# The attention's work list of a decoder trunk in segments: transposes, products with V and logits in twos, projection units behind them

## The chip, the cores and the metric

One core of a Trainium2 chip runs the whole trunk in one launch. The metric is the device time of one execution in microseconds (us). Of the kernel before there are three timed runs and one execution under the hardware profiler; the profile's times count from the start of its span.

## The reference

Two layers act on a residual stream `h` of 256 tokens by 1024 features in float32. Each layer is a half-step SwiGLU feed-forward, a token mixer and another half-step feed-forward, with RMS norms before and after each. Layer 0 mixes by a gated linear recurrence, layer 1 by an attention with forget gates, whose keys, values and gates come from the stream behind layer 0:

```python
def forgetting_attention(xq, w_q, w_o, k, v, c):
    q = (xq @ w_q).reshape(Bn, S, N_HEADS, HEAD_DIM).transpose(0, 2, 1, 3) * (HEAD_DIM ** -0.5)
    for blk in range(S // Q_BLOCK):
        ...
        logits = jnp.einsum('bhqd,bhkd->bhqk', q[:, :, q0:end], k[:, :, :end]).astype(jnp.float32)
        logits = logits + c[:, :, q0:end, None] - c[:, :, None, :end]
        ...
        p = jax.nn.softmax(logits, axis=-1).astype(v.dtype)
        outs.append(jnp.einsum('bhqk,bhkd->bhqd', p, v[:, :, :end]))
    ...
    return o @ w_o
```

There are 16 heads of 64, and two query blocks of 128 tokens: block 0 sees 128 keys, block 1 sees 256. Masking is causal. Every weight matrix is used once.

## The kernel before

The tokens stand in two tiles, 0 and 1, of 128 each. A float32 product is made of three products of rounded parts: each weight tile is split on its way in, its upper part by ScalarE (`whi`, line 173), the rest by VectorE (`wlo`, line 177), and TensorE then runs the three matmuls of lines 183 to 185 with 512 columns each. A weight tile of 128 by 1024 is an *item*: for each of the two token tiles it gives one *unit* of six such matmuls. SyncE issues the loads into five raw buffers; nine split tiles may exist at a time (`RAW`, `WB`). A helper, `prepare_next`, decides when an item's load and splits are written down, by estimated times and by how many items ahead they are.

TensorE's order is the order in which the program writes its instructions down (`manual_schedule` for that engine). The other engines' orders are chosen by the scheduler of the tile library, which takes instructions under `high_priority` first, unless one is held in program order.

In the attention of layer 1 this order is a list by hand, `ATT_ORDER` (line 1221), worked off at lines 1409 to 1415. An entry `0` or `1` is the next unit of that token tile: eight units a tile, in all, of the projection to Q (line 1209), with the four transposes that turn Q written two units later (`heads_T`, line 986), and then eight of the output projection (line 1211). An entry such as `l1` is the next step of the softmax of that token tile, made by `attention` (line 1129):

- `l`, `logits`: matmuls of K and Q on 64 rows (line 1151) into two banks, then on VectorE a reduction that adds the bias and finds the maximum (line 1160) and two small corrections (lines 1164, 1165), then on ScalarE the exponentials with their sums (line 1167). One call makes two groups; an odd call returns at once. A group is four heads of tile 0 or two heads of tile 1: 512 columns. I call the two groups of a call A and B.
- `n`, `norm`: on VectorE the reciprocal of the sums (line 1173) and the product with it (line 1174).
- `t`, `turn`: four transposes of a group on TensorE (line 1180) and a copy out of PSUM on ScalarE (line 1182).
- `v`, `values`: matmuls with V that fill 64 columns each (line 1194). With every eighth head the bank is read out by ScalarE (`oh`, line 1200) and VectorE (`ol`, line 1201); these feed the output projection.

Steps of the list are written down under `high_priority`. Logits use the two banks named `gt`, transposes the two named `tr`, V and the projections the four named `mm`. The last unit of a token tile's output projection is followed by `enter` (line 259): squares on ScalarE (line 205), the post-norm on VectorE (lines 272 and 285), both at high priority, and the next feed-forward's inputs by transposes of `h` (line 214).

## Time and profile before

| what | value |
|---|---|
| median of three runs | 985.26 us (984.47 to 985.72) |
| the profiled execution | 985.32 us, of which its span 983.6 us |
| TensorE matmuls | 975.0 us busy, 99% of the span |
| TensorE weight loads | 812.0 us, 83% |
| VectorE | 610.2 us, 62% |
| ScalarE | 528.1 us, 54% |
| GpSimd | 59.9 us, 6% |
| TensorE's granted clock over the span | 0.998 |

In the rows, PE is TensorE's matmuls, PEld its weight loads, DVE VectorE, ACT ScalarE, POOL GpSimd and SP SyncE. A timeline's row gives start, duration, engine, line, operation, output and inputs, shapes and count; matmuls overlap in the pipeline, so the distance of two starts tells more than a duration. A group's row gives after the bar the busy time in us, the mean of one in ns, and after the second bar the idle time of the engine just before these instructions. A float32 matmul on half of the array shows as two records.

### The profile page before, as it was taken

What the parts mean: (1) busy time and instruction counts of PE and PEld (TensorE: products, weight loads), DVE (VectorE), ACT (ScalarE), POOL (GpSimd) and SP (SyncE); (2) the same over time, 40 slices, a digit from 0 to 9 for tenths busy, and PEclk for the clock granted to TensorE, in tenths of its full rate; (3) what the DMA queues carried; (4) which work ended last, traced back from release to release, by engine and by line L of the source; (5) the groups of instructions that cost most, each with busy time, mean ns of one, the idle gap of its engine ahead of it and who ended that gap; (6) DMA issues with size and microseconds to landing.
All of it is one profiled execution on the core that took longest, in us unless ns stands there. A gap on an engine that the chain in (4) does not pass through costs nothing.

```text
span 983.6 us, 13267 instructions
## 1 busy us (share of the span) xinstructions
PE 975.0 (99%) x4863; PEld 812.0 (83%) x4863; DVE 610.2 (62%) x849; ACT 528.1 (54%) x749; POOL 59.9 (6%) x110
## 2 busy tenths in 40 slices
PE   9999999999999999999999999999999999999997
PEld 6888888898978888888899888888887788888886
DVE  6756554678997555554677455555487876555542
ACT  7545443568986544443555344444366855444431
POOL 2400000100002000000113000002020010000000
PEclk9999999999999999999999999999999999999999
DMA  8877665465346766665589767667772467666631
GB/s 290 276 256 245 226 212 192 151 201 162 113 129 201 237 212 209 219 206 189 131 178 307 238 211 214 213 216 237 220 252 85 131 204 235 214 212 214 208 114 43
DMA packets 102966, 196.84 MB, mean 200 GB/s; under 512 B 12974, under 2 KB 36886, under 8 KB 102774
## 3 DMA queue, kind: packets, MB, share of 16 engines
q1 hardware_dynamic: 100102, 188.95, 60.8%
q0 software_dynamic: 2192, 6.51, 2.3%
q8 instruction: 38, 0.62, 0.3%
q10 hardware_dynamic: 608, 0.53, 0.2%
q14 instruction: 26, 0.21, 0.1%
HBM read 182.32 MB, written 3.16 MB: 189 GB/s over the span
## 4 chain that ended last, share of the span: by engine, by line
PE 95%; DVE 2%; issue 2%; ACT 1%; DMA 0%; POOL 0%; POOLq 0%; ACTq 0%; DVEq 0%
PE mm L183 28%; PE mm L185 27%; PE mm L184 27%; PE mm L1023 2%; PE gt L761 2%; PE tr L525 1%; PE mm L1291 1%; PE mm L190 1%; PE mm L191 1%; PE mm L192 1%; DVE wlo L177 1%; PE gt L214 1%; ACT pe L1167 0%; DMA h<-in_x_dram 0%; PE mm L1194 0%
## 5 line engine op out<-in xcount | busy, mean ns | idle before, releaser
L177 DVE TENSOR_TENSOR wlo<-raw,whi 128x1024 fp32r<-128x1024 f32 (+5 forms) x329 | 395.8, 1208 | 265.6 <-ACT whi L173 263.5
L173 ACT ACTIVATE whi<-raw 128x1024 fp32r<-128x1024 f32 (+5 forms) x329 | 342.1, 1046 | 316.7 <-PE mm L185 245.7
L183 PE MATMUL mm<-whi,xhi 128*128 128x512 f32 (+1 forms) x768 | 301.1, 392 | 0.0
L185 PE MATMUL mm<-whi,xlo 128*128 128x512 f32 (+1 forms) x768 | 298.1, 388 | 0.3 <-DVE xlo L228 0.3
L184 PE MATMUL mm<-wlo,xhi 128*128 128x512 f32 (+1 forms) x768 | 298.0, 388 | 0.0
L185 PEld LDWEIGHTS mm<-whi,xlo 128*128 128x128 f32 x768 | 144.2, 188 | 30.7 <-DVE xlo L228 0.7
L183 PEld LDWEIGHTS mm<-whi,xhi 128*128 128x128 f32 x768 | 144.2, 188 | 30.1 <-issue 2.0
L184 PEld LDWEIGHTS mm<-wlo,xhi 128*128 128x128 f32 x768 | 144.3, 188 | 28.1 <-DVE wlo L177 0.3
L183 PE MATMUL mm<-whi,hhi 128*128 128x512 f32 x352 | 137.8, 392 | 0.0
L185 PE MATMUL mm<-whi,hlo 128*128 128x512 f32 x352 | 137.1, 389 | 0.0
L184 PE MATMUL mm<-wlo,hhi 128*128 128x512 f32 x352 | 137.0, 389 | 0.0
L185 PEld LDWEIGHTS mm<-whi,hlo 128*128 128x128 f32 x352 | 66.1, 188 | 13.7
L183 PEld LDWEIGHTS mm<-whi,hhi 128*128 128x128 f32 x352 | 66.1, 188 | 13.4
L184 PEld LDWEIGHTS mm<-wlo,hhi 128*128 128x128 f32 x352 | 66.1, 188 | 13.4
L510 DVE SCALAR_TENSOR_TENSOR prod<-mm,rstd,sil 128x512 f32<-128x512 f32 (+1 forms) x48 | 33.9, 706 | 39.4 <-PE mm L185 31.3
L498 ACT ACTIVATE sil<-mm,rstd 128x512 f32<-128x512 f32 (+1 forms) x48 | 31.2, 653 | 43.1 <-PE mm L185 34.8
L198 POOL TENSOR_SCALAR nv<-ss 128x1 f32<-128x1 f32 x22 | 9.7, 441 | 554.0 <-ACT junk L205 554.0
L529 ACT ACTIVATE hhi<-tr 128x512 fp32r<-128x512 f32 (+1 forms) x48 | 24.8, 558 | 13.2 <-PE tr L525 13.2
L205 ACT ACTIVATE junk<-mm 128x512 bf16<-128x512 f32 x24 | 14.3, 595 | 32.7 <-PE mm L185 32.7
L530 DVE TENSOR_TENSOR hlo<-tr,hhi 128x512 fp32r<-128x512 f32 (+1 forms) x48 | 29.2, 641 | 2.6 <-ACT hhi L529 2.6
L272 DVE TENSOR_TENSOR t<-mm,gb 128x512 f32<-128x512 f32 x24 | 16.2, 687 | 23.6 <-ACT junk L205 23.4
L190 PE MATMUL mm<-xhi,whi 128*126 128x256 f32 (+1 forms) x88 | 24.7, 281 | 0.0
(211 smaller groups left out, 918.6 us busy)
## 6 DMA issues: line engine op xcount, KB each, us to landing
raw<-in_ffn_w_down_dram SPq DMA_DIRECT2D x88, 512.0 KB
raw<-in_ffn_w_up_dram SPq DMA_DIRECT2D x80, 512.0 KB
raw<-in_ffn_w_gate_dram SPq DMA_DIRECT2D x78, 512.0 KB
prr<-prod SPq DMA_DIRECT2D x40, 256.0 KB
raw<-in_rg_w_in_dram SPq DMA_DIRECT2D x10, 504.0 KB
raw<-in_rg_w_out_dram SPq DMA_DIRECT2D x10, 504.0 KB
raw<-in_ffn_w_gate_dram SPq DMA_DIRECT2D x19, 256.0 KB
raw<-in_ffn_w_up_dram SPq DMA_DIRECT2D x16, 256.0 KB
```

What stands on the lines that cost most here:

```text
L173: up = nc.scalar.activation(hi[:parts, c:c + m], rawv[:, c:c + m], AF.Copy)
L177: nc.vector.tensor_tensor(lo[:parts, c:c + m], rawv[:, c:c + m], hi[:parts, c:c + m].bitcast(F32), ALU.subtract)
L183: nc.tensor.matmul(ps, xh, wh, start=first, stop=False)
L184: nc.tensor.matmul(ps, xh, wl, start=False, stop=False)
L185: nc.tensor.matmul(ps, xl, wh, start=False, stop=last)
L190: nc.tensor.matmul(ps, wh, xh, start=first, stop=False)
L498: nc.scalar.activation(s[:, :nn], ps, AF.Silu, scale=rs[t][:, 0:1])
L510: nc.vector.scalar_tensor_tensor(pr[:, :nn], ps, rs[t][:, 0:1], s, ALU.mult, ALU.mult)
L529: nc.scalar.activation(hv, tp[:, :nn], AF.Copy)
L530: nc.vector.tensor_tensor(lv, tp[:, :nn], hv.bitcast(F32), ALU.subtract)
L761: nc.tensor.matmul(ps[j][:w, g * S:(g + 1) * S], wv[rows, o:o + w], xc[rows, k, :], start=start, stop=stop, skip_group_check=True)
L1023: nc.tensor.matmul(ps[:, j * S:(j + 1) * S], w, x, start=k == 0 and j == 0 and i == 0, stop=k == 7 and i == 2, skip_group_check=True)
```

## The change

Only the list is another; the entries are as many of each kind as before.

```diff
-    ATT_ORDER = ("0 0 0 0 0 0 0 l0 0 1 n0 l0 1 1 t0 n0 1 l0 v0 1 t0 n0 l0 1 v0 n0 1 t0 l1 1 v0 t0 n1 l1 0 v0 "
-                 "n1 l1 t1 0 n1 l1 t1 0 n1 l1 v1 v1 t1 0 n1 l1 t1 0 n1 l1 v1 v1 t1 0 n1 l1 t1 0 n1 v1 v1 0 t1 1 "
-                 "t1 v1 1 v1 1 1 1 1 1 1")
+    ATT_ORDER = ("0 0 0 0 0 0 0 l0 l0 0 1 1 n0 1 n0 1 t0 t0 l0 l0 1 1 n0 1 n0 1 t0 t0 v0 v0 l1 l1 0 n1 0 n1 "
+                 "t1 t1 v0 v0 l1 l1 0 n1 0 n1 t1 t1 v1 v1 l1 l1 0 n1 0 n1 t1 t1 v1 v1 l1 l1 0 n1 0 n1 "
+                 "t1 t1 v1 v1 1 1 v1 v1 1 1 1 1 1 1")
```

A segment of the new list is: two transposes, two steps with V, two entries of logits, then projection units with the two norms among them. In the middle of the list a step with V belongs to groups that were transposed one segment earlier.

## The prediction

> **What bounds the kernel now.** I read the page first, then the groups of the attention's stretch, then the stretches by engine, then the timelines of TensorE, VectorE and ScalarE side by side. The page says what the end hangs on:

> ```profile
> span 983.6 us, 13267 instructions
> ...
> PE 95%; DVE 2%; issue 2%; ACT 1%; DMA 0%; POOL 0%; POOLq 0%; ACTq 0%; DVEq 0%
> ```

> The chain that ended last is TensorE for 95% of the span. The groups of lines between 724 and 792 us, where the attention's list is worked off, show whether the steps that the change moves ever hold TensorE up (last column: idle time just before them):

> ```profile
> L1180 PE MATMUL tr<-ident,pe 128*128 128x128 f32 x48 | 7.4, 277 | 0.0
> L1194 PE MATMUL mm<-pT,v 128*64 128x128 f32 x96 | 7.3, 283 | 0.0
> L1151 PE MATMUL gt<-kT,qT 64*128 64x256 f32 x32 | 4.5, 402 | 0.0
> ```

> They never do: the 48 transposes, the products with V and the logits waited 0.0 us in total. The other engines are not idle there, though. In the ten microseconds from 765 the columns are length, then busy time of TensorE, its weight loads, VectorE, ScalarE and GpSimd:

> ```profile
> 765.00:775.00 10.00, 10.00 (x79) 7.89 (x76) 10.00 (x31) 8.54 (x18) 0.00 (x0) 1.00 0.60 192
> ```

> VectorE is busy for all ten, ScalarE for 8.54, and yet TensorE does not stop. So this stage is bound by TensorE's own instruction stream, and the softmax on the two other engines is hidden behind it because the list leaves it time. There are two ways for a new order to move the time: TensorE's stream itself gets shorter, or the cover of the softmax is lost.

> **Part 1: what TensorE's stream gains.** The order list decides TensorE's order alone, and the counts stay as they are. I take the price of a change between full-array work and work on half the array (logits: 64 rows, V: 64 columns) from a V step that stands alone, and of transposes from a lone one:

> ```profile
> 775.14 0.40 PE L185 MATMUL mm<-whi,ol 128*128 128x512 f32 x1
> 775.47 1.20 PE L1194 MATMUL mm<-pT,v 128*64 128x128 f32 x16
> 776.60 0.50 PE L183 MATMUL mm<-whi,oh 128*128 128x512 f32 x1
> 776.93 0.40 PE L184 MATMUL mm<-wlo,oh 128*128 128x512 f32 x1
> ...
> 777.86 0.39 PE L185 MATMUL mm<-whi,ol 128*128 128x512 f32 x1
> 778.09 0.60 PE L1180 MATMUL tr<-ident,pe 128*128 128x128 f32 x4
> 778.45 0.48 PE L183 MATMUL mm<-whi,oh 128*128 128x512 f32 x1
> 778.76 0.39 PE L184 MATMUL mm<-wlo,oh 128*128 128x512 f32 x1
> ```

> From 777.86 to 778.76 are two projection products (0.227 each, the pitch of 777.86 to 778.09) and four transposes: 0.90 - 0.454 = 0.446, or 0.11 a transpose. Transposes mixed in among products cost nothing beyond themselves. From 775.14 to 776.93 are two products and eight matmuls with V (sixteen records): 1.79 - 0.454 = 1.336; at 0.109 each the eight take 0.87, so a stretch of half-array work pays about 0.46 for going in and out. The 0.33 from 776.60 to 776.93, 0.10 more than a product's pitch, is part of it. TensorE's order before has eleven such stretches, after it eight, with four seams between V and logits inside them both times. Three fewer at 0.4 to 0.46: **-1.3 us**. Grouping the transposes in twos gains nothing. The two `l` entries that now stand together are one step as before, since the odd one returns at once.

> [...]

> **Part 2: what the softmax loses.** With two groups A and B of a logits step, the list of before puts the transposes of A behind the next logits step, those of B another unit later. One step of token tile 1, in the three engines:

> ```profile
> 752.59 1.14 PE L1151 MATMUL gt<-kT,qT 64*128 64x256 f32 x8
> 753.65 0.50 PE L183 MATMUL mm<-whi,xhi 128*128 128x512 f32 x1
> ...
> 759.46 0.66 PE L1180 MATMUL tr<-ident,pe 128*128 128x128 f32 x4
> ...
> 761.77 0.60 PE L1180 MATMUL tr<-ident,pe 128*128 128x128 f32 x4
> ```
> ```profile
> 753.06 0.69 DVE L1174 TENSOR_TENSOR pe<-pe,sm 128x512 f32<-128x512 f32 x1
> 753.75 0.43 DVE L1160 CUSTOM_DVE_ANT_0 pe<-gt,bias 128x256 f32<-128x256 f32 x1
> ...
> 756.91 0.69 DVE L1174 TENSOR_TENSOR pe<-pe,sm 128x512 f32<-128x512 f32 x1
> 758.17 0.17 DVE L1173 RECIPROCAL sm<-sm 128x2 f32<-128x2 f32 x1 [0.57 <-ACT pe L1167]
> 758.37 0.69 DVE L1174 TENSOR_TENSOR pe<-pe,sm 128x512 f32<-128x512 f32 x1
> ```
> ```profile
> 756.58 0.58 ACT L1182 ACTIVATE pT<-tr 128x512 f32<-128x512 f32 x1
> 757.06 0.50 ACT L1167 ACTIVATE pe<-pe,mx 128x256 f32<-128x256 f32 x1
> ```

> The logits start at 752.59 and end at 753.73; VectorE's first reduction starts at 753.75, 1.16 after the logits began. A is ready at 756.91 + 0.69 = 757.60, 3.85 after that first reduction, so 5.01 after the logits began. Its transposes came at 759.46: 1.86 to spare. B is ready at 758.37 + 0.69 = 759.06, its transposes came at 761.77: 2.71 to spare. That slack is the cover.

> In the new list every step of tile 1 reads: two transposes, two V, logits, then `0 n1 0 n1`, then the transposes of these same logits. Between logits and transposes stand two units of six products. TensorE reaches them 1.06 (752.59 to 753.65) + 0.33 + 11 x 0.227 = **3.89** after the logits began, against 5.01. The built order confirms that VectorE still does reductions A, B, A, B and ScalarE exponentials A, A, B, B, but now without the copy of a transposed tile (756.58 to 757.06, 0.48) between A and B, so B is ready 759.06 - 757.60 - 0.48 = 0.98 after A. By segment:

> - A segment with nothing in the way (the third of tile 1): A waits 5.01 - 3.89 = 1.12. Then come 0.45 of transposes; B waits 0.98 - 0.45 - 0.10 = 0.43. I add 0.1 for each wait, for the pipeline that has to fill again (nearest row: the 0.10 behind the V step above; bounds 0 and 0.3). Sum **1.8**.
> - The second segment: a V step that completes four heads' pairs stands right before the logits, and its evacuation stands ahead of the reductions in VectorE's order. In before it took this:

> ```profile
> 758.51 0.60 ACT L1200 ACTIVATE oh<-mm 128x512 fp32r<-128x512 f32 x1 [0.37 <-PE mm L1194]
> ```
> ```profile
> 759.14 0.69 DVE L1201 TENSOR_TENSOR ol<-mm,oh 128x512 fp32r<-128x512 f32 x1
> 759.75 0.41 DVE L1160 CUSTOM_DVE_ANT_0 pe<-gt,bias 128x256 f32<-128x256 f32 x1
> ```

>   From 758.51 to 759.75 are 1.24 us, against the 1.14 that the logits take meanwhile: the reductions start 0.1 to 0.25 later. Sum **2.0**.
> - The first segment of tile 1 has the same evacuation but four more transposes (of Q, 0.45) as cover: **1.5** Its first output products also need that evacuation: the third of them starts 1.06 + 0.33 + 0.23 = 1.6 after the logits began, the evacuation ends about 1.3 after V, or 1.8 behind one more copy. That is 0 to 0.2, of which I take nothing, since a wait there shortens the next by as much.
> - The fourth segment: the two units of tile 0 in it are that tile's last, so its squares and its post-norm go, at high priority, between the exponentials. The built order has exp A, square, exp A, square, exp B, exp B on ScalarE, and the post-norm's passes around both normalisations on VectorE:

> ```profile
> 777.80 0.57 ACT L205 ACTIVATE junk<-mm 128x512 bf16<-128x512 f32 x1
> ```
> ```profile
> 778.73 1.28 DVE L272 TENSOR_TENSOR t<-mm,gb 128x512 f32<-128x512 f32 x2
> 780.26 1.42 DVE L285 SCALAR_TENSOR_TENSOR h<-t,rstd,h 128x512 f32<-128x512 f32 x2 [0.25 <-POOL rstd L200]
> ```

>   A: 1.12 + 0.4 (evacuation, behind a copy) + 0.6 (a square) + 0.1 = 2.2. B: ScalarE's second pair, then a pass of 0.64, the reciprocal's 0.20, a pass of 0.71 and the normalisation's 0.69 on VectorE come to about 2.05 after A; less 0.55, 1.5. Sum with 0.2: **3.9**.
> - The last step of tile 0 (four units and Q's transposes as cover):

> ```profile
> 744.45 1.16 PE L1151 MATMUL gt<-kT,qT 64*128 64x128 f32 x16
> ```

>   In before its B was ready at 753.06 + 0.69 = 753.75, 9.3 after the logits began, with a copy and an evacuation of about 0.97 on ScalarE among its exponentials that no longer stand there: 8.3. TensorE comes at 1.1 + 0.33 + 23 x 0.227 + 0.9 = 7.5. B waits up to 0.8, and 0.4 if VectorE starts earlier: **0.7** with refill; A does not wait.

> Waits: 0.7 + 1.5 + 2.0 + 1.8 + 3.9 = **+9.9**. Queued behind each waiting transpose on TensorE are the other transposes, the V step, the next logits and all later products; nothing can pass. The other engines see only a later start of the next segment, so a wait is not made good in the next one. The first step (tile 0, thirty products and Q's transposes behind it) and the V steps, which come a segment after their transposes, wait for nothing.

> SyncE's list of loads and GpSimd's list are the same instructions in the same order, renamed; a load leaves when VectorE has split the tile before it. I cost this at nothing, because weights run up to nine units ahead here; if that cover is gone, it is the second rival.

> **Sum**: +9.9 - 1.3 = +8.6. The profiled execution took 985.3 with its span of 983.6, and the median of the runs is 985.26, the same to 0.1: 985.3 + 8.6 = **993.9**.

> **The rivals.**

> 1. *Part of it stays hidden.* B's waits vanish under the transposes of A and the post-norm of tile 0 slips behind the exponentials as in before. Then A alone waits: 0.9 + 1.3 + 1.1 + 1.5, plus 0.4 refill, = 5.2, less 1.3: +3.9, **989.2**. For it: the scheduler's priorities held in before. Against: the built order has the square between the exponentials.
> 2. *Weights come late afterwards.* VectorE splits weights between softmaxes, and a softmax on which TensorE waits pushes the splits back:

> ```profile
> L177 DVE TENSOR_TENSOR wlo<-raw,whi 128x1024 fp32r<-128x1024 f32 x17 | 20.6, 1220 | 1.8 <-ACT whi L173 1.7
> ```

>    Seventeen splits of 1.22 fall in this stretch. If three of those are missing when TensorE enters the next feed-forward: +3.4 to +3.7 more, **997.4**. For it: VectorE's 10.00 of 10 from 765. Against: TensorE's waits give VectorE the time back.
> 3. *TensorE's clock falls in the waits.* Granted clock is 1.00 in the row from 765. A product at half the clock takes 0.227 more; twelve of them 2.7 us, and two segments so hit add 5.4: **999.3**. Nothing in this trace speaks for it, since TensorE never stops in this stage. [...]
> 4. *Not slower: the softmax fits into twelve products.* Place: logits to the transposes of A. It decides from 3.85 after the first reduction down to 3.89 - 1.16 = 2.73, which must hold in all segments; then only the gain is left, -1.3: **984.0**. For it: ScalarE and VectorE are freed of copies in between. Against: the 3.85 is a chain of dependent steps in which only one foreign step stood, and that one behind A.

> That the change doesn't do what it says is excluded by the built order, which has V and logits joined and transposes in pairs.

> **How the numbers follow.** Forecast 0.72, rival 1 0.14, rival 2 0.07, rival 3 0.03, rival 4 0.04. The forecast itself spreads from 991 (no refill, B half hidden) to 997 (refill 0.3, evacuations in full). To leave out no more than 2 in 10 the range takes in rivals 1 and 2: 988.5 to 998.5. A difference of 0.2% (2 us) is about what can be told from no change. Rival 4 is within it, with a little of rival 1's low end: same 0.05; faster 0.01; slower 0.94.

> **What would show it.** In the profile after: TensorE's idle time before the transposes of line 1180, 0.0 now, becomes 8 to 9 us, released by VectorE's normalisation of line 1174, with the largest waits in the last segment before tile 0's post-norm. Half-array stretches are eight. From the next feed-forward on, TensorE has no idle time again and runs the same distance later. I am wrong if the transposes' idle time is under 4 us, if TensorE waits for weights after the attention, or if the granted clock leaves 1.00.

## The result, and the profile after

| what | before | after |
|---|---|---|
| median of four timed runs each, on one chip | 985.18 us (984.47 to 985.72) | 995.83 us (994.18 to 997.20) |
| ratio to before, 95% interval | | 1.0106 [1.0093, 1.0118] |
| the profiled execution, its span | 985.32 us, 983.6 us | 997.20 us, 995.5 us |
| TensorE's granted clock over the span | 0.998 | 0.994 |

The new list is 10.65 us slower where I forecast 8.6. The first lines of the page of the kernel after, its row of the granted clock in 40 slices, and its chain of waits:

```profile
span 995.5 us, 13265 instructions
...
PEclk9999999999999999999999999999999899999999
...
PE 93%; DVE 2%; ACT 2%; issue 1%; DMA 0%; POOL 0%; POOLq 0%; ACTq 0%; DVEq 0%
```

TensorE still sets the end, with 93% of the chain. One slice of the clock's row stands at 8: the slice from 771 to 796 us, the end of the attention's list. The groups between 724 and 803 us, with the three lines of the attention on TensorE:

```profile
L1180 PE MATMUL tr<-ident,pe 128*128 128x128 f32 x48 | 7.7, 290 | 7.8 <-ACT pe L1167 4.9 <-DVE pe L1174 2.2 <-ACT whi L173 0.7
L1194 PE MATMUL mm<-pT,v 128*64 128x128 f32 x96 | 8.0, 318 | 0.0
L1151 PE MATMUL gt<-kT,qT 64*128 64x256 f32 x32 | 5.5, 469 | 0.0
```

The transposes, which waited for nothing before, wait 7.8 us; V and logits still wait for nothing. But two means rose that no wait explains: a matmul with V from 283 to 318 ns, one of the logits from 402 to 469 ns. TensorE's timeline shows both effects, in the first segment of tile 1 and in the last (the bracket is the idle time just before a row):

```profile
753.88 1.13 PE L1151 MATMUL gt<-kT,qT 64*128 64x256 f32 x8
...
759.27 0.63 PE L1180 MATMUL tr<-ident,pe 128*128 128x128 f32 x4 [0.80 <-ACT pe L1167]
760.26 0.63 PE L1180 MATMUL tr<-ident,pe 128*128 128x128 f32 x4 [0.35 <-DVE pe L1174]
760.81 1.09 PE L1194 MATMUL mm<-pT,v 128*64 128x128 f32 x16
...
784.96 0.63 PE L1180 MATMUL tr<-ident,pe 128*128 128x128 f32 x4 [1.96 <-ACT pe L1167]
787.16 1.08 PE L1180 MATMUL tr<-ident,pe 128*128 128x128 f32 x4 [1.57 <-DVE pe L1174]
788.17 1.98 PE L1194 MATMUL mm<-pT,v 128*64 128x128 f32 x16
...
790.67 0.63 PE L184 MATMUL mm<-wlo,oh 128*128 128x512 f32 x1
791.10 0.63 PE L185 MATMUL mm<-whi,ol 128*128 128x512 f32 x1
```

The waits stand before the transposes of A and of B, as forecast. Behind the last one everything is slow: the step with V takes 1.98 instead of 1.09, and from product to product are 0.43 (790.67 to 791.10) instead of 0.23. That is half the clock. In this stage the clock changed at 769.14, 772.55, 786.21 and 793.03: 3.41, 13.66 and 6.82 us apart, which is one, four and two times 3.41 to 3.42. In windows of that length the columns are length, busy time of TensorE, its weight loads, VectorE, ScalarE and GpSimd, granted clock, DMA share and GB/s:

```profile
765.73:769.14 3.41, 1.82 (x17) 1.26 (x18) 2.79 (x5) 3.41 (x9) 0.00 (x0) 1.00 0.00 0
769.14:772.55 3.41, 3.41 (x23) 2.26 (x18) 1.57 (x3) 0.80 (x2) 0.00 (x0) 0.50 0.59 161
772.55:775.97 3.42, 2.88 (x12) 2.01 (x11) 2.29 (x14) 1.78 (x7) 0.00 (x0) 1.00 0.50 146
...
782.79:786.21 3.42, 0.84 (x5) 0.42 (x4) 2.73 (x6) 3.13 (x11) 1.09 (x2) 1.00 0.27 104
786.21:789.62 3.41, 2.46 (x18) 2.16 (x20) 1.46 (x3) 1.35 (x3) 0.00 (x0) 0.50 0.00 0
789.62:793.03 3.41, 3.41 (x13) 2.50 (x10) 0.00 (x0) 0.29 (x2) 0.79 (x2) 0.50 0.00 0
793.03:796.45 3.42, 3.42 (x26) 2.54 (x26) 2.09 (x2) 2.69 (x3) 0.00 (x0) 1.00 0.03 6
```

Three windows were run at a clock of 0.50, each behind one in which TensorE had been idle: 3.41 - 1.82 = 1.59 us, 3.42 - 0.84 = 2.58, and 3.41 - 2.46 = 0.95 in a window that was itself at half clock. They last 10.24 us, 0.95 of it idle, so the slow clock cost (10.24 - 0.95) / 2 = 4.65 us in this execution.

To put the terms side by side I measure one **stretch** in each kernel, from the first logits to the last transposes of `h`. What lies behind it is 983.6 - 799.00 = 184.6 us before and 995.5 - 810.85 = 184.65 after. Ahead of the stretch the kernel after ran 0.60 shorter (it begins at 734.77, before at 735.37); the two lists are the same up to there, and in the runs below the start lies anywhere from 734.77 to 736.65. So all of the loss lies in the stretch. The stretch as one window, before and after:

```profile
735.37:799.00 63.63, 63.55 (x410) 49.36 (x410) 52.24 (x148) 46.58 (x114) 3.63 (x8) 1.00 0.46 146
```
```profile
734.77:810.85 76.08, 68.24 (x410) 53.01 (x410) 53.06 (x148) 46.55 (x114) 3.86 (x8) 0.93 0.40 124
```

It grew by 12.45 us: 7.76 more idle time (7.84 against 0.08), 4.65 of slow clock, and 0.04 that is left over for all other terms together. At full clock the new list would so cost 12.45 - 4.65 = 7.80 us of stretch.

### The profile page after: what moved, and what is told of

Read it like the earlier page. It is cut to its first block, busy times and chain, and to the rows that moved or that the text cites. A ratio compares the mean times of both kernels' runs of the same rounds, so it can differ in the third digit from the quotient of the medians.

```text
span 995.5 us, 13265 instructions
## 1 busy us (share of the span) xinstructions
PE 979.7 (98%) x4863; PEld 815.7 (82%) x4863; DVE 610.4 (61%) x849; ACT 528.2 (53%) x749; POOL 61.1 (6%) x110
## 4 chain that ended last, share of the span: by engine, by line
PE 93%; DVE 2%; ACT 2%; issue 1%; DMA 0%; POOL 0%; POOLq 0%; ACTq 0%; DVEq 0%
PE mm L183 27%; PE mm L185 27%; PE mm L184 27%; PE mm L1023 2%; PE gt L761 2%; PE tr L525 1%; PE mm L1291 1%; PE mm L190 1%; PE mm L191 1%; PE mm L192 1%; ACT pe L1167 1%; DVE pe L1160 1%; PE mm L1194 1%; PE gt L214 1%; DVE wlo L177 0%
## 5 line engine op out<-in xcount | busy, mean ns | idle before, releaser
L177 DVE TENSOR_TENSOR wlo<-raw,whi 128x1024 fp32r<-128x1024 f32 (+5 forms) x329 | 395.0, 1207 | 277.0 <-ACT whi L173 274.7
L173 ACT ACTIVATE whi<-raw 128x1024 fp32r<-128x1024 f32 (+5 forms) x329 | 341.8, 1046 | 322.5 <-PE mm L185 249.0
L183 PE MATMUL mm<-whi,xhi 128*128 128x512 f32 (+1 forms) x768 | 300.8, 392 | 0.0
L185 PE MATMUL mm<-whi,xlo 128*128 128x512 f32 (+1 forms) x768 | 298.1, 388 | 0.3 <-DVE xlo L228 0.3
L184 PE MATMUL mm<-wlo,xhi 128*128 128x512 f32 (+1 forms) x768 | 298.0, 388 | 0.0
L185 PEld LDWEIGHTS mm<-whi,xlo 128*128 128x128 f32 x768 | 144.2, 188 | 30.7 <-DVE xlo L228 0.7
L183 PEld LDWEIGHTS mm<-whi,xhi 128*128 128x128 f32 x768 | 144.2, 188 | 29.8 <-issue 1.3
L184 PEld LDWEIGHTS mm<-wlo,xhi 128*128 128x128 f32 x768 | 144.3, 188 | 28.2 <-DVE wlo L177 0.3
L183 PE MATMUL mm<-whi,hhi 128*128 128x512 f32 x352 | 137.8, 392 | 0.0
L185 PE MATMUL mm<-whi,hlo 128*128 128x512 f32 x352 | 137.1, 389 | 0.0
L184 PE MATMUL mm<-wlo,hhi 128*128 128x512 f32 x352 | 137.0, 389 | 0.0
L185 PEld LDWEIGHTS mm<-whi,hlo 128*128 128x128 f32 x352 | 66.1, 188 | 13.9
L184 PEld LDWEIGHTS mm<-wlo,hhi 128*128 128x128 f32 x352 | 66.1, 188 | 13.4
L183 PEld LDWEIGHTS mm<-whi,hhi 128*128 128x128 f32 x352 | 66.1, 188 | 13.2
L205 ACT ACTIVATE junk<-mm 128x512 bf16<-128x512 f32 x24 | 14.2, 594 | 32.8 <-PE mm L185 32.8
L272 DVE TENSOR_TENSOR t<-mm,gb 128x512 f32<-128x512 f32 x24 | 16.2, 686 | 24.5 <-ACT junk L205 24.4
```

The costliest lines, as they stand in the source:

```text
L173: up = nc.scalar.activation(hi[:parts, c:c + m], rawv[:, c:c + m], AF.Copy)
L177: nc.vector.tensor_tensor(lo[:parts, c:c + m], rawv[:, c:c + m], hi[:parts, c:c + m].bitcast(F32), ALU.subtract)
L183: nc.tensor.matmul(ps, xh, wh, start=first, stop=False)
L184: nc.tensor.matmul(ps, xh, wl, start=False, stop=False)
L185: nc.tensor.matmul(ps, xl, wh, start=False, stop=last)
```

## The experiments

My theory, once the result was seen: the new list costs the waits that I forecast, and the waits cost a second time through the clock. Rivals: the waits alone, with the rest due to the joining of V and logits; or the slow clock as a disturbance that has nothing to do with the list. In every kernel the time behind the stretch was 184.6 to 184.7 us (span less the stretch's end), so the stretch is what I compare. Each row of the table is one profiled execution. The two executions of the new list differ by 0.21 in the rest, so a rest of a few tenths from a single execution is not firm. The ratios below are to runs of before taken beside each kernel: their median is 986.24 us for experiments 1, 2, 3 and 6, and 985.81 for 4, 5, 7 and 8.

| kernel | stretch | idle | time at half clock (idle in it) | stretch less before: idle + clock + filler + rest |
|---|---|---|---|---|
| after | 76.08 | 7.84 | 10.24 (0.95) | 12.45: 7.76 + 4.65 + 0 + 0.04 |
| the new list again | 73.43 | 7.92 | 3.41 (0) | 9.80: 7.84 + 1.71 + 0 + 0.25 |
| transposes behind the logits | 63.03 | 0.42 | 0 | -0.60: 0.34 + 0 + 0 - 0.94 |
| V before the transposes | 69.68 | 4.90 | 3.41 (0.47) | 6.05: 4.82 + 1.47 + 0 - 0.24 |
| waits filled | 71.82 | 1.48 | 0 | 8.19: 1.40 + 0 + 6.58 + 0.21 |
| three waits filled | 71.87 | 3.93 | 0 | 8.24: 3.85 + 0 + 4.31 + 0.08 |
| one unit less of cover | 84.46 | 12.37 | 17.07 (1.11) | 20.83: 12.29 + 7.98 + 0 + 0.56 |
| post-norm not urgent | 69.99 | 6.06 | 0 | 6.36: 5.98 + 0 + 0 + 0.38 |
| V and logits parted | 63.50 | 0.50 | 0 | -0.13: 0.42 + 0 + 0 - 0.55 |

Idle is the length of the stretch less TensorE's busy time in it; the clock's cost is half of the time at half clock that was not idle; a filler is counted at the 0.227 of a product (five of them took 1.26 us in experiment 3, 0.38 of it the last: 0.22 each).

**1. The transposes behind the logits.** The segments stay, with V and logits joined, but the transposes go behind the next logits, and those of the last step a unit later each:

```diff
-... n0 1 n0 1 t0 t0 v0 v0 l1 l1 0 n1 0 n1 t1 t1 v0 v0 l1 l1 0 n1 0 n1 t1 t1 v1 v1 l1 l1 ...
+... n0 1 n0 1 v0 v0 l1 l1 t0 t0 0 n1 0 n1 v0 v0 l1 l1 t1 t1 0 n1 0 n1 v1 v1 l1 l1 t1 t1 ...
-... t1 t1 v1 v1 1 1 v1 v1 ...
+... v1 v1 1 t1 1 t1 v1 v1 ...
```

> The new list's grouping is kept (V and logits side by side, transposes and logits in twos), but the transposes of a logits step stand behind the next logits step, one segment later, as in the old list; at the end of the list the last V step is moved a unit forward to keep its evacuation covered. My theory (the loss is TensorE waiting for the softmax, plus the clock that falls in these waits; the grouping itself gains 1.3 us): idle time before the transposes under 1.5 us, clock 1.00 through the stage, 983.5 to 985.5. Rival (the grouping itself costs, by longer stretches on half the array or by evacuations that come in pairs): it stays at 990 or more.

Measured: 985.64 us against 986.24, ratio 0.9995 [0.9986, 1.0003], 0.14 above the range I expected. The attention's waits on TensorE in this kernel (what waited, for whom: us in total, times, longest), and its stretch:

```profile
PE mm L1194 <- ACT pT L1182: 0.2, 1, 0.2
PE tr L1180 <- DVE pe L1174: 0.2, 1, 0.2
```
```profile
735.96:798.99 63.03, 62.61 (x411) 49.76 (x411) 52.38 (x148) 46.47 (x114) 3.98 (x8) 1.00 0.48 147
```

With the cover back, 0.4 us of the 7.8 remain, the clock stays at 1.00, and the stretch is 0.60 shorter than before. So the loss lies in the place of the transposes and not in the joined V and logits. The grouping is a gain, but only of 0.94 us net of idle time, and the median cannot tell it from nothing: this order is better than the new list, and not shown to be better than before.

**2. V before the transposes.** Only the order within a segment is changed, so V's 1.02 us come to stand between logits and transposes:

```diff
-... t1 t1 v0 v0 l1 l1 0 n1 0 n1 t1 t1 v1 v1 l1 l1 ...
+... v0 v0 t1 t1 l1 l1 0 n1 0 n1 v1 v1 t1 t1 l1 l1 ...
```

> The new list with one step moved inside each segment: the V step (1.0 us) stands before the transposes, not behind them, so that it covers the softmax too. My theory: TensorE's wait for group A falls by about 1.0 in each segment of tile 1 (from 0.80, 1.24, 0.93 and 1.96 to about 0, 0.2, 0 and 1.0), B's stay at 0.2 to 0.4 with about 1.5 in the last segment; idle before transposes 3 to 5 us, the clock falls at most once: 988 to 991. Rival (the order of transposes, V and logits on TensorE is what costs, not the cover): 994 or more.

Measured: 991.47 us, ratio 1.0060 [1.0045, 1.0076]. The idle time fell to 4.90, but the time is a little over what I expected. The last segment is the miss: A waited 2.72 there. TensorE's row, then VectorE's and ScalarE's of that softmax:

```profile
782.53 0.86 PE L1180 MATMUL tr<-ident,pe 128*128 128x128 f32 x4 [2.72 <-DVE sm L1173]
```
```profile
777.26 0.15 DVE L1164 TENSOR_TENSOR mx<-mx,cq 128x2 f32<-128x2 f32 x1
777.33 1.22 DVE L177 TENSOR_TENSOR wlo<-raw,whi 128x1024 fp32r<-128x1024 f32 x1
778.47 0.15 DVE L1165 TENSOR_TENSOR mx<-mx,cq 128x2 f32<-128x2 f32 x1
...
780.60 0.15 DVE L1173 RECIPROCAL sm<-sm 128x2 f32<-128x2 f32 x1
781.03 0.75 DVE L285 SCALAR_TENSOR_TENSOR h<-t,rstd,h 128x512 f32<-128x512 f32 x1 [0.28 <-POOL rstd L200]
781.70 0.69 DVE L1174 TENSOR_TENSOR pe<-pe,sm 128x512 f32<-128x512 f32 x1
```
```profile
778.79 0.50 ACT L1167 ACTIVATE pe<-pe,mx 128x256 f32<-128x256 f32 x1
```

Two things stood in the way. A weight split of 1.22 us slipped in between the two small corrections of the maximum, and the exponentials could only start behind it: they start 4.08 us after the logits (774.71 to 778.79), against 3.19 in the kernel after (778.92 to 782.11). Then a pass of tile 0's post-norm (line 285) went ahead of A's normalisation, which starts 1.10 after its reciprocal here and 0.19 after it in the kernel after (rows further down). Together these are 1.8 us, about what A waited beyond the 1.0 that I expected. Both are choices of VectorE's order by the scheduler, which the list does not fix; no run isolates them. The window with the wait (from 779.38, 2.72 us idle) was followed by one at a clock of 0.50 (from 782.79).

**3. The waits filled, the clock kept.** Useless bf16 products into the transposes' bank stand before the transposes of tile 1, about as many as the wait was long:

```diff
+FILL = {(1, 0): 3, (1, 1): 1, (1, 2): 5, (1, 3): 1, (1, 4): 4, (1, 5): 1, (1, 6): 8, (1, 7): 6}
...
+            for _ in range(FILL.get((t, hg), 0)):
+                nc.tensor.matmul(tp, nc.const_aps.tensor(1.0, (P, P), BF16), nc.const_aps.tensor(1.0, (P, 512), BF16),
+                                 start=True, stop=True)
```

> The new list unchanged, but matmuls of constants, whose result is thrown away, fill TensorE's waits: before the transposes of tile 1's eight groups stand 3, 1, 5, 1, 4, 1, 8 and 6 of them, 512 columns each. They do work that nothing needs. If the clock falls because TensorE idles: granted clock 1.00 through the stage and 991 to 993, faster than the new list by its two slow windows (about 4 us) although it does more. If the clock falls for another reason (its own rhythm, the load): still two slow windows and 995 to 998.

Measured: 994.61 us (993.59 to 998.58), ratio 1.0092 [1.0075, 1.0110]; the profiled execution 993.59. The stretch:

```profile
735.42:807.24 71.82, 70.34 (x439) 52.45 (x439) 53.02 (x148) 46.54 (x114) 3.85 (x8) 1.00 0.42 130
```

The clock stayed at 1.00 through the stage and the stretch came out 4.26 us shorter than in the profiled execution after, though TensorE did 29 products more. That is near the 4.65 that I put down to the clock. The median misses what I expected by 1.6 us, since I had set what is left without the slow clock too low. By the stretch it is 8.2 us. One of the four runs took 998.58 at a mean clock of 0.997, where the others have 0.998 and 0.999; it was not profiled, and a clock lower by 0.001 to 0.002 is worth 1 to 2 us of the 4 that it is longer, so the rest stays open.

**4. Three waits filled.** Fillers only before the three longest waits, to see whether those alone bring the slow windows:

```diff
+FILL = {(1, 2): 5, (1, 6): 8, (1, 7): 6}
```

> The new list, with matmuls of constants (work that nothing needs) in three places only: before the transposes of A in the second segment of tile 1 (5) and before A and B in the last (8 and 6). The profiles so far show a slow window behind a stretch of 3.41 us that held 1.59 us of idle time or more, and none behind 0.97 or less; the waits that stay unfilled (0.80 + 0.35 and 0.93 + 0.36, less than 1.3 in any such stretch) lie between. If idle time in the stretch before decides: no slow window, or at most one, and 1 to 4 us less than the new list of the same call. If any wait of about 1 us brings the clock down: two or more slow windows as in the new list, and no gain.

Measured: 994.18 us (994.03 to 994.65), ratio 1.0079 [1.0066, 1.0091]; 2.2 us less than the 996.39 of the new list run beside it (experiment 5), as expected.

```profile
735.87:807.74 71.87, 67.94 (x427) 51.66 (x429) 53.02 (x148) 46.52 (x114) 3.85 (x8) 1.00 0.41 128
```

The same stretch as with all waits filled, and no slow window, though 3.9 us of idle time remain. Its five runs lie within 0.6 us. So in these runs the clock fell with the long waits: with those of 1.24, 1.96 and 1.57 us filled it stayed at 1.00. The 0.97 of the expectation holds for windows at full clock; behind half windows with 0.95 (786.21 after) and 0.78 us idle (771.19 in experiment 6) the next was at half too. What the new list costs at full clock is 7.8 to 8.2 us of stretch: 7.80 by the kernel after, 8.09 by experiment 5 less its clock, 8.19 and 8.24 with fillers.

**5. The new list again**, without an edit, beside the runs before and after it:

> The new list itself, unchanged, once more, on the chip and beside the runs of the three kernels sent with it, so that they can be compared. Theory: from the first logits to the last transposes of h the profile shows about 76 us against 63.6 in the list of before, made of about 7.8 us of idle time and half of the 3 to 10 us in which the clock is at half; the time is 993 to 997 and moves between executions with the number of slow windows. Rival (a fixed cost, the same in every execution): the runs agree within 1 us whatever the clock.

Measured: 996.39 us (994.04 to 998.37), ratio 1.0099 [1.0082, 1.0115]. Its waits are those of the first profile (7.9 us idle). The clock is not: only one window fell.

```profile
767.22:770.64 3.42, 1.83 (x13) 1.06 (x11) 2.42 (x5) 3.42 (x11) 0.00 (x0) 1.00 0.00 0
770.64:774.05 3.41, 3.41 (x31) 2.64 (x31) 3.02 (x9) 1.17 (x2) 0.00 (x0) 1.00 0.49 135
774.05:777.46 3.41, 2.29 (x12) 1.44 (x10) 2.15 (x10) 2.85 (x9) 0.00 (x0) 1.00 0.54 172
...
784.29:787.70 3.41, 0.76 (x5) 0.58 (x6) 3.25 (x8) 2.05 (x7) 1.09 (x2) 1.00 0.00 0
787.70:791.11 3.41, 3.41 (x22) 2.66 (x22) 0.39 (x1) 1.63 (x3) 0.71 (x2) 0.50 0.00 0
791.11:794.53 3.42, 3.42 (x28) 2.67 (x26) 1.04 (x1) 1.84 (x2) 0.08 (x1) 1.00 0.01 2
```

Two executions with the same waits thus differ by 4.65 - 1.71 = 2.9 us in clock alone. One of the two windows between them comes from where the last waits fall: after, they are spread over two windows (2.58 us idle, then 0.95 at half clock), here they lie in one (3.41 - 0.76 = 2.65). The other is not explained: a window with 1.59 idle was followed by half clock there (765.73) and not here (767.22). The whole executions differ by only 0.8 us, since this one reached its stretch 1.88 later. This list's five runs go with it: the mean clock is 0.998 at 994.04 us and 0.994 at 998.37. The clock need not be all of this spread of 4.3 us, since the nine runs of before beside them spread over 3.9.

**6. One unit less of cover.** One of the two units between logits and transposes goes behind V:

```diff
-... l1 l1 0 n1 0 n1 t1 t1 v1 v1 l1 l1 ...
+... l1 l1 0 n1 n1 t1 t1 v1 v1 0 l1 l1 ...
```

> The new list with one of the two units (1.36 us) of each segment of tile 1 moved from before the transposes to behind the V step: the cover is halved. My theory: A's wait grows by 1.36 to 1.4 in each of the first three segments; in the last the post-norm no longer stands in the way, so about 2.4 and 0.4; idle before transposes 10.5 to 12.5. With the clock falling behind each stretch that has more than about 1.6 us of idle time in 3.4: 1001 to 1005; with the clock of the new list's two windows, 999. Rival (the cover does not matter): 996, as the new list.

Measured: 1005.69 us, ratio 1.0193 [1.0179, 1.0207], 0.7 above the range I expected; the idle time, 12.37 us, is within it. Two of its windows of TensorE:

```profile
791.67:795.08 3.41, 0.95 (x6) 0.42 (x4) 2.15 (x10) 2.08 (x8) 0.00 (x0) 1.00 0.00 0
795.08:798.49 3.41, 3.08 (x21) 2.45 (x21) 0.18 (x1) 1.19 (x2) 0.00 (x0) 0.50 0.01 2
```

The idle time rose by 4.5 us for about 1.36 us (six products) of cover taken from each of four segments, 5.4 in all, and every segment now brought a slow window, one of them two: 17.07 us at half clock. Waits and clock grow together, which a disturbance from elsewhere would not do.

**7. The post-norm not urgent.** Only the priority of tile 0's post-norm is taken away; the list is the new one:

```diff
-        urgent = tc.high_priority()
+        urgent = nullcontext() if calm else tc.high_priority()
...
-              lambda t, accs: enter(t, [main_dest(GI[("ffn2", 1)], t)], accs, gbox["mix1"], False, wait=4),
+              lambda t, accs: enter(t, [main_dest(GI[("ffn2", 1)], t)], accs, gbox["mix1"], False, wait=4, calm=t == 0),
```

> The new list, but the post-norm of tile 0 in the attention is written down without high priority, so that its squares and passes go behind the exponentials and normalisations of the last segment; nothing else changes. My theory of the last segment (post-norm between the softmax's steps): its two waits fall from 1.96 and 1.57 to about 1.3 and 0.4, so 2 us less idle, and the slow windows behind it shrink: 2 to 4 us less than the new list of the same call. Rival (the last segment is late for another reason, the splits or the evacuation): the waits stay above 3 us together.

Measured: 992.14 us, ratio 1.0063 [1.0042, 1.0084]; 4.25 less than the new list beside it, a little more than I expected. The last segment on TensorE:

```profile
784.17 0.63 PE L1180 MATMUL tr<-ident,pe 128*128 128x128 f32 x4 [1.27 <-ACT pe L1167]
785.15 0.63 PE L1180 MATMUL tr<-ident,pe 128*128 128x128 f32 x4 [0.35 <-DVE pe L1174]
```

It waited 1.62 us instead of 3.53, and in this execution no window fell. So of the last segment's wait 1.91 us are the post-norm between the exponentials and the normalisations, as the prediction had it. It still waits 6.06 us in the whole stretch, so this edit mends a part only.

**8. V and logits parted again.** Against experiment 1, one unit stands between V and logits in three segments:

```diff
-... v0 v0 l1 l1 t1 t1 0 n1 0 n1 v1 v1 l1 l1 t1 t1 0 n1 0 n1 ...
+... v0 v0 0 l1 l1 t1 t1 0 n1 n1 v1 v1 0 l1 l1 t1 t1 0 n1 n1 ...
```

> The list with transposes one segment later, with one unit moved between V and logits in three of the segments, so that three joined stretches on half the array become six. It prices the first part of the change, three stretches fewer. By my price (0.46 for a stretch alone, a seam about 0.15): from the first logits to the last transposes of h 63.9 us against 63.0 for the joined list, with idle time below 0.8 in both. If joining is worth nothing: 63.0.

One run: 984.66 us, stretch 63.50, half-way between the two values. Net of idle time that is 0.39 us more than in experiment 1, or 0.13 for each pair parted. Each parting adds a stretch on half the array and takes away a seam (the place where V and logits meet inside a stretch), so 0.13 is the price of a stretch less that of a seam; the 0.15 that I expected for a seam was an estimate. It is too small for the time of a whole run to show.

## Why the prediction was right in its waits and lacked a term

**The waits (+9.9 with refill).** Right in mechanism, place and nearly in size. The releaser needs a second look. The rows name ScalarE's exponentials before A's transposes; VectorE's and ScalarE's rows of the last segment after show the order in time:

```profile
783.93 0.16 DVE L1173 RECIPROCAL sm<-sm 128x2 f32<-128x2 f32 x1
784.12 0.69 DVE L1174 TENSOR_TENSOR pe<-pe,sm 128x512 f32<-128x512 f32 x1
784.73 0.68 DVE L272 TENSOR_TENSOR t<-mm,gb 128x512 f32<-128x512 f32 x1
...
785.66 0.75 DVE L285 SCALAR_TENSOR_TENSOR h<-t,rstd,h 128x512 f32<-128x512 f32 x1
786.33 0.68 DVE L1174 TENSOR_TENSOR pe<-pe,sm 128x512 f32<-128x512 f32 x1
```
```profile
782.11 0.51 ACT L1167 ACTIVATE pe<-pe,mx 128x256 f32<-128x256 f32 x1 [2.48 <-DVE mx L1165]
782.53 0.18 ACT L1167 ACTIVATION_READ_ACCUMULATOR pe<-pe,mx 128x1 f32 x1
782.62 0.58 ACT L205 ACTIVATE junk<-mm 128x512 bf16<-128x512 f32 x1
...
784.65 0.19 ACT L1167 ACTIVATION_READ_ACCUMULATOR pe<-pe,mx 128x1 f32 x1
```

A is normalised at 784.12 + 0.69 = 784.81, and its transposes start at 784.96; B at 786.33 + 0.68 = 787.01, and they start at 787.16. So it is the normalisation both times, 0.15 us ahead. The exponential that ends close by (its sum is read out at 784.65 + 0.19 = 784.84) stands behind A's reciprocal of 783.93, so it belongs to B and could not release A. The square and the passes of the post-norm stand where the built order had them. Against the forecast, without refill:

| segment | A and B forecast | A and B measured (idle) |
|---|---|---|
| last step of tile 0 | 0, 0.7 with refill | 0.28 in all |
| first of tile 1 | 1.5 with refill in all | 0.80, 0.35 |
| second | 2.0 with refill in all | 1.24, 0.35 |
| third | 1.12, 0.43 | 0.93, 0.36 |
| fourth | 2.2, 1.5 | 1.96, 1.57 |

Together 7.84 against 9.0 without the nine refills of 0.1. (The 2.2 holds a 0.1 that the prediction does not name; if that is a refill, one was counted twice and it is 8.9.) In the fourth segment there is some luck: the four pieces that I named for B, 0.64, 0.20, 0.71 and 0.69, add up to 2.24 and not to 2.05. The runs show 787.01 - 784.81 = 2.20, so the right sum would have given B 1.7 instead of 1.5. Tile 0's step and the second and third segments were each set a little too long, by 0.2 to 0.3. The evacuation before the reductions is visible: in the first segment A was ready 759.12 - 753.88 = 5.24 after the logits, where I had 5.01 and 0.1 to 0.25 more. The output products that could have waited for it wait for nothing, as costed. Refill was close too: the rest column of the runs with the new list (after, experiments 5 and 7), +0.04 to +0.38, plus the 0.94 gained by the grouping, leaves 1.0 to 1.3 for nine waits, 0.11 to 0.15 each. This is a remainder and no experiment isolates it, but the rows show where it can sit: a wait is counted as idle only when the last product's 0.39 us are over, 0.16 after the next one would have begun at the pitch of 0.227. In the second segment the transposes start 767.18 - 761.84 = 5.34 after the logits, 1.45 behind the 3.89 of cover, and 1.24 of that show as idle.

**The gain of TensorE's stream (-1.3).** The size was about 0.4 too large, if all of experiment 1's rest is put down to it: 0.94 for three half-array stretches fewer, 0.31 each. I had read 0.46 from one lone step, and that row was a long one: in the kernel after, a lone step with V takes 794.07 to 795.75 = 1.68 where I had 1.79, and the same working gives 0.36. Parting three of the pairs again cost only 0.13 each in experiment 8. The two agree if a stretch costs 0.31 and a seam 0.18, since a parting takes a seam away. But the list of experiment 8 has eleven stretches like before and still ends 0.55 below it, net of idle time; whether its three seams fewer gain this, or something else that it shares with experiment 1, such as the transposes in twos, no run separates.

**Rival 1 and rival 2** did not happen. B waits in all four segments, and the post-norm does stand between. TensorE has nothing more to wait for behind the attention: the time behind the stretch is 184.65 against 184.6.

**Rival 3, the clock.** This is the step that failed. I gave it 0.03, since nothing in this stage of the trace of before spoke for it; and I named the clock leaving 1.00 as a sign that I was wrong. It left 1.00. The priced size was good (5.4 for two segments, against 4.65 in the profiled execution), but it was an estimate: half the clock over twelve products in each of two segments was shown by no run. What the runs showed is a clock of 0.50 in windows of 3.41 us (772.55 - 769.14), three of them after and one in experiment 5. The end of the trace of before has half clock too, from 980.16 behind 2.68 us idle, but it does not show how little is enough, and the prediction takes each wait by itself. No single wait after was over 1.96 us. The waits of A and B that fall into one window made 2.58 us of idle time in the last segment. My own forecast held this: with waits of 2.2 and 1.5 and 0.5 of transposes between, 3.41 us can be idle for up to 2.9. In the kernel after the clock fell from 1.00 to 0.50 behind windows with 1.59 and 2.58 us idle of 3.41.

**The sum.** Without the clock the new list costs 7.8 to 8.2 us of stretch, against 8.6 forecast; idle time set 1.2 too high was partly offset by a stream gain 0.4 too large and a refill 0.1 to 0.4 too low. Experiment 4, which keeps the clock, took 8.4 us more than before beside it. The clock adds 1.7 us in one profiled execution of the list and 4.65 in the other, and the new list beside experiment 4 took 2.2 more: that is the excess of the median over the forecast. That the median still lies within 988.5 to 998.5 is partly luck: the room above the forecast had been left for weights that come late, and the clock used it.

## What to carry to other kernels

When an order written by hand groups steps, compare for each pair of producer and consumer the work that stands between them with the length of the chain on the other engines; here 3.89 us of cover stood against 5.0 to 5.2 of softmax, and the grouping itself was worth less than 1 us. Count TensorE's idle time also by the windows of 3.41 us at whose ends the clock changed here: two waits of 1.96 and 1.57 that lie together cost 2.9 us more in clock in one execution, and nearly the same two 1.7 us in the other. Where a stall can't be avoided, moving other urgent work out of it can be worth more than the length of that work: in experiment 7 1.9 us less idle time made the stretch 3.4 to 6.1 us shorter.

## What the runs showed of the hardware that was not expected

The ends of the two kernels, where TensorE's last product is followed by one long idle stretch, narrow this further. After, the window from 987.60 with 1.68 us idle in one piece was followed by one more at full clock, and that one, idle for all of its 3.41 us, by a half one from 994.42. Before, the window from 976.75 with 2.68 us idle was followed by half clock at 980.16. So no single threshold of idle time fits all rows: 1.59 was enough once, 1.68 was not. The sum over a window fits better than its longest piece: the window from 784.29 in experiment 5, with 2.65 us idle, was followed by half clock, though no piece in it was over 1.6: its waits are 1.9 and 1.6, and 0.86 us of the first lie in the window before.

Behind half windows less idle time went with another half one: with 0.95 (786.21 after) and 0.78 (771.19 in experiment 6) the next stayed at half, with 0.47 (782.79 in experiment 2) and 0.33 (795.08 in experiment 6) it was full again.
